# Padding three SBUF pools so that every tile that a matmul reads starts at a multiple of 256 bytes

## The chip, the cores and the metric

The kernel runs on 1 core of a Trainium2 chip. The metric is the device time of one execution in microseconds (us): 1028.81 us in the median of 3 runs (1028.7 to 1029.01). TensorE's clock has two levels, 1.2 and 2.4 GHz, which the profile shows as a granted clock of 0.5 and 1.0.

## The reference, cut to what matters

One layer of an encoder trunk on 512 tokens of width 1024, in float32, followed by a last RMSNorm. Every large product is a dense matmul:

```python
x = x + hybrid_mixer(rms_norm(x, norm_mix_g[l]), ...)          # p = h @ w_in (1024 x 7168), three gated branches, @ w_out
x = x + memory_cross_attention(rms_norm(x, norm_xa_g[l]), mem, ...)  # 4 heads of 256 into 256 memory tokens
x = x + swiglu(rms_norm(x, norm_ffn_g[l]), ...)                # (silu(h @ w_gate) * (h @ w_up)) @ w_down, hidden width 2816
return rms_norm(x, final_g)
```

## The kernel before, in words

A float32 product is made of three passes in the type float32r. An operand v is kept as two float32r tiles, hi (v rounded) and lo = v - hi, and `gemm` (L129 to L135) issues hi*hi, hi*lo and lo*hi into one PSUM tile. Each pass is a matmul with a 128x128 stationary operand, loaded by a weight load of its own (PEld in the profile), and a moving operand that streams 128 rows by N columns, N being 512 nearly everywhere. A moving column is 4 bytes in each of the 128 partitions, so a moving operand of 512 columns is a run of 2048 bytes in each partition, and a stationary one a run of 512.

The work goes through these stages, in program order, and TensorE's order is the program's:

- load and first norm, the values v of the attention (matmuls `pv`, N = 256);
- q and k (`pq`), the convolution branch (`pc`) and the attention heads (`z`), interleaved;
- the spatial gating (`pn`), then the gated branches (`pgt` and `pbr`);
- the projection back (`pb`, class `Back`), keys and values of the memory (`pk`, N = 256, and `pn`), cross attention (`pq`, `sc` with N = 256, `po`), `pb` again;
- the feed-forward part: the first columns with N = 256 (`pf`), then `pfg` and `pfu`, then `pb` for the down projection.

There are two forms of these products. In `col_gemm` (L137: `pq`, `pc`, `pgt`, `pfg`, `pfu`, `pk`, `pf`) a piece of a weight (`wh`, `wl`) is stationary and activations (`hT`, `h2`, `h3`, `mT`) move. In `nat_gemm` (L142: `pn`) and `Back` (L543 on: `pb`) activations (`hT`, `mT`, `mt`, `oT`, `aT`) are stationary and a weight piece of [128, 2, 512] moves. Transposes (L191, L401, L687, L498) are matmuls of 128 columns in plain float32, whose moving operand is the constant `ident`.

A weight is loaded by one DMA of SP's queue into a raw tile (`load_raw`, L107, two buffers) and split by ACT (hi, L100) and DVE (lo, L101) into `wh` and `wl`, five buffers each (`cut`, L112). These loads and splits run ahead of TensorE.

SBUF is given out by tile pools. Pools without a side are a stack that grows from low addresses, those with `side="right"` a stack that grows down from the top. Each tile takes its bytes in each partition, rounded up to a multiple of 32. The order of the pools on the left is `cst` (constants), `wp` (weights), `sm` (statistics), then the pools of each stage, opened and closed as the work goes on. `cst` starts at byte 16,512, and its tiles take 512 (`ident`), 32 (`mhalf`, one element), 512 (`zero`) and 192 (`chan`) bytes; so `wp` starts at 17,760, which is 96 bytes past a multiple of 256. `wp` takes 57,344 bytes, a multiple of 256, and `sm` 1,344, so that what follows starts at 76,448, 160 past one. The right side ends 32 bytes below the end of SBUF, at 229,344, and its tiles start 224 past a multiple of 256. Every address that a matmul reads keeps these remainders, as the steps inside the tiles are multiples of 512 bytes:

| tiles | bytes past a multiple of 256 |
|---|---|
| `wr`, `wh`, `wl` (weights) | 96 |
| `hT`, `h2`, `h3`, `mT`, `kx`, `vx`, `ya`, `yb`, `yc`, `vv`, `qk`, `kh`, `vl`, `ws` | 160 |
| `mt`, `oT`, `aT`, `qx`, `pT`, `es` (right side) | 224 |
| `ab`, `ah`, `al` (after the 1,284-column tile `om` in the pool `sk`) | 192 |
| `ident` | 128 |

In the pool `sk`, two tiles have a width that isn't a multiple of 64 elements: `om` (ZC + 4 = 1,284 columns, L382) and `y` (T + 2 = 514 columns, L355).

The instructions' order is made by the tile framework from the program and the tiles' dependencies. A tile that lies where a closed pool's tile lay waits for the last use of that one.

Of the kernel before, what the change touches and what calls it, by code (L numbers as in the profile page):

```python
# [17 lines left out]
def encoder_kernel(  # L18
# [6 lines left out]
):  # L25
    """Float32 products run as float32r passes: an operand v is kept as hi, v rounded to 12
    significant bits, and lo = v - hi, which is exact; hi*hi + hi*lo + lo*hi."""
    nc = tc.nc
# [36 lines left out]

# [1 line left out]
    ident = cst.tile([P, P], F32, name="ident")  # L67
# [4 lines left out]
    nc.vector.memset(zero, 0.0)  # L72
    # per-channel vectors, a row tile of 128 channels a column: four norm gains, three conv taps; spatial biases
    NC_ = 4 * KD + 3 * CT + CT
    WARM = 24
    chan = cst.tile([P, NC_], F32, name="chan")
    G_MIX, G_XA, G_MEM, G_FFN, C_W, B_S = 0, KD, 2 * KD, 3 * KD, 4 * KD, 4 * KD + 3 * CT

# [1 line left out]
    psx = {"i": 0, "pools": [(ps, "mm", 2)]}  # L80
# [16 lines left out]
    def split(src, hi, lo, scale=None):  # L97
        """hi = src rounded to float32r, lo = src - hi."""
        if scale is None:
            nc.scalar.copy(out=hi, in_=src)  # L100
            nc.vector.tensor_tensor(out=lo, in0=src, in1=hi, op=ALU.subtract)  # L101
        else:
            nc.scalar.activation(out=hi, in_=src, func=AF.Copy, scale=scale)
            nc.vector.scalar_tensor_tensor(out=lo, in0=src, scalar=scale, in1=hi,
                                           op0=ALU.mult, op1=ALU.subtract)
# [12 lines left out]
    def w_cols(w, c0, k0=0, k=KD, n=256):  # L118
        """Stationary weight: rows k0*128.., columns c0..c0+n, as n/128 tiles [128, k, 128]."""
        raw = load_raw(w[k0 * P:(k0 + k) * P, c0:c0 + n].rearrange("(k p) n -> p k n", p=P), k, n)  # L120
        return [cut(raw, (slice(None), slice(None), slice(j * P, (j + 1) * P)), k, P)
                for j in range(n // P)]

    def w_rows(w, k0, k, c0):
        """Moving weight: k row tiles from k0, 512 columns, as k/2 tiles [128, 2, 512]."""
        raw = load_raw(w[k0 * P:(k0 + k) * P, c0:c0 + 512].rearrange("(k p) n -> p k n", p=P), k, 512)
        return [cut(raw, (slice(None), slice(2 * j, 2 * j + 2)), 2, 512) for j in range(k // 2)]

    def gemm(dst, lh, ll, rh, rl, ks, first=True, last=True):  # L129
        """dst += sum over k of (lh+ll)[k].T @ (rh+rl)[k]; ks: pairs of indices."""  # L130
        n, tot = 0, 3 * len(ks)
        for a, b in ((lh, rh), (lh, rl), (ll, rh)):
            for i, j in ks:
                nc.tensor.matmul(dst, a(i), b(j), start=first and n == 0, stop=last and n == tot - 1)  # L134
                n += 1  # L135

    def col_gemm(dst, w, act, cs, k=KD):  # L137
        """dst[n, t] = w.T @ act: w = (hi, lo) [128, k, 128], act = (hi, lo) [128, k, T]."""
        gemm(dst, lambda i: w[0][:, i, :], lambda i: w[1][:, i, :],
             lambda i: act[0][:, i, cs], lambda i: act[1][:, i, cs], [(i, i) for i in range(k)])  # L140

    def nat_gemm(w, col0, act, ntt, evac):  # L142
        """out[t, n] for 512 columns of w."""
        pieces = []
        for c in range(2):
            pieces += w_rows(w, 4 * c, 4, col0)
        for t in range(ntt):
            dst = bank(nm("pn"))
            gemm(dst,
                 lambda i: act[0][:, i, t * P:(t + 1) * P], lambda i: act[1][:, i, t * P:(t + 1) * P],  # L150
                 lambda i: pieces[i // 2][0][:, i % 2, :], lambda i: pieces[i // 2][1][:, i % 2, :],
                 [(i, i) for i in range(KD)])
            evac(t, dst)
# [13 lines left out]
    def square_half(np_, key, xt, half):  # L167
        """Sum of squares of a half of a token tile's channels; with the second half, both summed."""
        junk = np_.tile([P, 512], F32, name=nm("jk"), tag="jk")
# [15 lines left out]
    def norm_turn(np_, h, g0, dst, t):  # L185
        """Transposes a token tile, applies the gain, splits into dst[:, :, token tile t]."""
        for g in range(2):
# [9 lines left out]

    # ================= mixer =================
    hp = pool("hp")
# [4 lines left out]
    sb = pool("sb")  # L204
    # v of a head: 64 columns hi, 64 columns lo
    vv = sb.tile([P, NT, W // HD, 2, HD], F32R, name="vv")
# [51 lines left out]

    # keeps the tensor engine's clock up while the first loads are under way
    warm = bank("warm")  # L260
# [32 lines left out]

    # key blocks (transposed) and query blocks (natural), packed to 1280 columns without crossing a bank
    OFF = {0: 0, 1: 512, 3: 896, 2: 1024}
    QOF = {3: 0, 2: 512, 0: 896, 1: 1024}
    ZC = 1280
    # one where no factor stands between s and t: s >= t - 1
    emask = sk.tile([P, ZC], F32, name="emask")
# [10 lines left out]
    def qk_jobs(c, got):  # L310
        """q and k, transposed, of two head pairs: four jobs."""
        held = {}

        def job(which, j):
# [3 lines left out]
            col_gemm(dst, held[which][j], hT, ALLT)  # L318
            # of the two heads in dst, each with its hi part on its own rows of qs, lo on the other head's;
            # ks the other way round, so that one product of 128 rows gives hi*lo + lo*hi  # L320
            st = sk.tile([P, 2, T], F32R, name=nm("qk"), tag=f"qk{which}", bufs=2)
# [17 lines left out]
    def conv_jobs(c):  # L339
        """The convolution branch for 256 channels: six jobs."""  # L340
        held, ccs, tmps = {}, [], []

        def job(which, j):
# [10 lines left out]
            elif which == 1:  # L354
                y = sk.tile([P, T + 2], F32, name=nm("y"), tag="y", bufs=1)  # L355
                nc.gpsimd.memset(y[:, 0:2], 0.0)
                nc.vector.tensor_tensor(out=y[:, 2:], in0=dst, in1=ccs[j], op=ALU.mult)
                tm = sk.tile([P, T], F32, name=nm("tm"), tag="tm", bufs=2)
                nc.scalar.activation(out=tm, in_=y[:, 2:], func=AF.Copy, scale=tap(2))
                nc.vector.scalar_tensor_tensor(out=tm, in0=y[:, 1:T + 1], scalar=tap(1), in1=tm,  # L360
# [12 lines left out]
    def sb_weights(par, q, k):  # L373
        """a[t, s] of a head, query block by query block: sig(z_ts) times the product of 1 - sig(z_tj), s < j < t."""
        r = HEAD[par]
        z = psz.tile([P, 1536], F32, name=nm("z"), tag="z", bufs=2)
        for i, o in QOF.items():
# [3 lines left out]
            mm(z[:, o:o + n], q[0][:, par, qi], k[0][:, par, 0:n], False, True)  # L381
        om = sk.tile([P, ZC + 4], F32, name=nm("om"), tag="om", bufs=1)  # L382
        nc.gpsimd.memset(om[:, ZC:ZC + 4], 1.0)
# [13 lines left out]
    def sb_turn(z, ab):  # L397
        """a transposed, key block by key block, in two parts."""
        for i in range(NT):
# [8 lines left out]
    def sb_values(pair, par, z, ah, al):  # L408
        r = HEAD[par]
        n_ = 0  # L410
        for i in range(NT):
            st = vv[:, i, 2 * pair + par].rearrange("p a d -> p (a d)")
            for b in (ah, al):
                mm(z[:, i * P:512], st, b[:, OFF[i]:OFF[i] + (NT - i) * P], n_ == 0, n_ == 2 * NT - 1)
                n_ += 1
        # v hi's rows and v lo's rows, summed
        yl = sk.tile([P, T], F32, name=nm("yl"), tag="yl", bufs=1)
# [32 lines left out]

# [1 line left out]
    yb_p = pool("ybp")  # L452
# [32 lines left out]
    for g in range(CT):  # L485
        gs = slice(g * P, (g + 1) * P)
        dst = bank(nm("pg")).rearrange("p (n c) -> p n c", n=NT)
        gemm(dst, lambda i: ws[0][:, g, :], lambda i: ws[1][:, g, :],
             lambda i: vl[0][:, :, gs], lambda i: vl[1][:, :, gs], [(0, 0)])
        # (mixed + bias) * u, in place of u  # L490
        nc.vector.scalar_tensor_tensor(out=un[:, :, gs], in0=dst, scalar=chan[:, B_S + g:B_S + g + 1],
                                       in1=un[:, :, gs], op0=ALU.add, op1=ALU.mult)
# [10 lines left out]

# [1 line left out]
    mtp = pool("mtp", side="right")  # L505
# [32 lines left out]

    # ================= residual, projections back to the model width =================
    xp = pool("xp")  # L540
    xr = [xp.tile([P, D], F32, name=f"xr{t}") for t in range(NT)]

    class Back:  # L543
        """xr[t] += act.T @ w. Halves of 512 columns; in the second one the last `tail` row tiles go
        token tile by token tile."""

# [81 lines left out]

    # memory keys and values
    for c in range(4):  # L630
# [12 lines left out]

    # ================= cross attention =================
    op_ = pool("op", side="right")
# [78 lines left out]

    # ================= feed forward =================
    # the first 256 columns start with the first two token tiles
    HT = (slice(0, T // 2), slice(T // 2, T))
# [55 lines left out]
    close(psm)  # L783
    close(ps)
    close(sm)
    close(wp)
# [30 lines left out]
```

## Time and profile before

| | |
|---|---|
| median of 3 runs | 1028.81 us (1028.7 to 1029.01) |
| profiled execution, its own time (span from the first to the last instruction) | 1028.6 us |
| PE, PEld, DVE, ACT, POOL busy | 98%, 81%, 44%, 37%, 8% of the span |
| DMA | 100.65 MB, mean 98 GB/s |
| granted clock of TensorE, mean | 0.994 |

How to read it: PE is TensorE's matmuls, PEld its weight loads, which overlap the matmuls. A matmul's end is modelled, and its duration holds the time in the pipeline, so the mean duration of a matmul (some 390 ns) isn't the time that it takes from the next one; that is the distance between starts, which the chain of waits gives for a run of equal matmuls as its length divided by its count.

### The profile page before, as it was taken

The numbers are of one execution on the slowest core, as the hardware profiler recorded it, in microseconds if no ns is written. First come the engines' busy times: TensorE is split into PE (matmuls) and PEld (weight loads), VectorE is DVE, ScalarE is ACT, GpSimd is POOL, SyncE is SP. The second block draws the span as 40 slices with busy tenths as digits, with TensorE's granted clock in tenths as the row PEclk, the third lists the DMA queues.
The fourth block names the chain that finished last, engine by engine and source line by source line (L and its number), as shares of the span: only waits on it lengthen the run. The fifth ranks groups of instructions, "written<-read, shape, count | busy, mean of one in ns | idle before, by whom it ended". The sixth has DMA issues, their size and how long they took to land.

```text
span 1028.6 us, 11686 instructions
## 1 busy us (share of the span) xinstructions
PE 1012.3 (98%) x4826; PEld 836.7 (81%) x4826; DVE 454.5 (44%) x576; ACT 381.7 (37%) x541; POOL 86.2 (8%) x115
## 2 busy tenths in 40 slices
PE   7999999999999999999999999999999999999997
PEld 7978778887888888888888887988888888888885
DVE  6576687545332323346745443643333333322213
ACT  5464554334222223345534433542332322312211
POOL 1121122130001212120000000000000000000000
PEclk8999999999999999999999999999999999999999
DMA  7312212123223232360544121232322322323202
GB/s 246 116 59 72 82 50 100 46 83 123 83 80 123 83 123 64 101 244 25 182 137 149 41 82 41 83 124 84 121 82 86 120 82 87 120 81 122 82 21 83
DMA packets 77334, 100.65 MB, mean 98 GB/s; under 512 B 1905, under 2 KB 57249, under 8 KB 77281
## 3 DMA queue, kind: packets, MB, share of 16 engines
q1 hardware_dynamic: 76032, 95.45, 28.4%
q0 software_dynamic: 1248, 4.46, 1.2%
q8 instruction: 38, 0.62, 0.3%
q14 instruction: 16, 0.12, 0.0%
HBM read 97.80 MB, written 2.10 MB: 97 GB/s over the span
## 4 chain that ended last, share of the span: by engine, by line
PE 95%; DMA 1%; ACT 1%; DVE 1%; issue 1%; SPq 0%; POOL 0%; DVEq 0%; POOLq 0%; ACTq 0%
PE pb L134 20%; PE pgt L134 13%; PE pfg L134 11%; PE pfu L134 11%; PE pq L134 8%; PE pn L134 7%; PE pc L134 6%; PE pbr L134 6%; PE z L371 3%; PE pv L134 2%; PE pf L134 2%; PE pk L134 1%; PE po L134 1%; PE sc L134 1%; PE pt L191 1%; PE z L401 1%
## 5 line engine op out<-in xcount | busy, mean ns | idle before, releaser
L101 DVE TENSOR_TENSOR wl<-wr,wh 128x1024 fp32r<-128x1024 f32 x174 | 213.1, 1229 | 304.2 <-ACT wh L100 150.9
L100 ACT CAST wh<-wr 128x1024 fp32r<-128x1024 f32 x174 | 181.2, 1048 | 369.6 <-PE pb L134 87.4
L134 PE MATMUL pb<-wh,aTh 128*128 128x512 f32 x176 | 55.2, 395 | 0.0
L134 PE MATMUL pb<-wl,aTh 128*128 128x512 f32 x176 | 55.2, 395 | 0.0
L134 PE MATMUL pb<-wh,aTl 128*128 128x512 f32 x176 | 55.2, 395 | 0.0
L759 DVE TENSOR_TENSOR fs<-pfu,fs 128x512 f32<-128x512 f32 x20 | 13.8, 692 | 85.4 <-PE pfu L134 85.4
L134 PE MATMUL pgt<-hTh,wh 128*128 128x512 f32 x192 | 47.9, 392 | 0.0
L134 PE MATMUL pgt<-hTl,wh 128*128 128x512 f32 x192 | 47.9, 392 | 0.0
L134 PE MATMUL pgt<-hTh,wl 128*128 128x512 f32 x192 | 47.8, 391 | 0.0
L162 POOL TENSOR_TENSOR rs<-ve,mhalf 128x1 f32<-128x1 f32 x22 | 14.4, 657 | 381.8 <-DVE ve L160 369.4
L531 POOL TENSOR_TENSOR merged<-merged,sg 128x512 f32<-128x512 f32 x16 | 27.7, 1731 | 184.8 <-DVE sg L530 184.8
L134 PEld LDWEIGHTS pgt<-hTh,wl 128*128 128x128 f32 x192 | 36.1, 188 | 8.0
L134 PEld LDWEIGHTS pgt<-hTl,wh 128*128 128x128 f32 x192 | 36.1, 188 | 7.9
L134 PEld LDWEIGHTS pgt<-hTh,wh 128*128 128x128 f32 x192 | 36.0, 188 | 7.9 <-DVE ybl L101 0.2
L134 PE MATMUL pfg<-h3h,wh 128*128 128x512 f32 x160 | 40.0, 391 | 0.0
L134 PE MATMUL pfg<-h3l,wh 128*128 128x512 f32 x160 | 39.9, 392 | 0.0
L134 PE MATMUL pfu<-h3l,wh 128*128 128x512 f32 x160 | 39.9, 392 | 0.0
L134 PE MATMUL pfu<-h3h,wh 128*128 128x512 f32 x160 | 39.9, 391 | 0.0
L134 PE MATMUL pfu<-h3h,wl 128*128 128x512 f32 x160 | 39.8, 391 | 0.0
L134 PE MATMUL pfg<-h3h,wl 128*128 128x512 f32 x160 | 39.8, 391 | 0.0
L134 PEld LDWEIGHTS pb<-wh,aTh 128*128 128x128 f32 x176 | 33.0, 188 | 8.1
L134 PEld LDWEIGHTS pb<-wh,aTl 128*128 128x128 f32 x176 | 33.0, 188 | 8.0
(240 smaller groups left out, 1824.6 us busy)
## 6 DMA issues: line engine op xcount, KB each, us to landing
wr<-in_w_in_dram SPq DMA_DIRECT2D x26, 1024.0 KB, 5.1
wr<-in_w_gate_ffn_dram SPq DMA_DIRECT2D x11, 1024.0 KB, 5.4
wr<-in_w_up_ffn_dram SPq DMA_DIRECT2D x11, 1024.0 KB, 5.3
wr<-in_w_down_ffn_dram SPq DMA_DIRECT2D x10, 1024.0 KB, 4.9
wr<-in_w_branch_dram SPq DMA_DIRECT2D x6, 1024.0 KB, 5.2
wr<-in_w_out_dram SPq DMA_DIRECT2D x4, 1024.0 KB, 5.0
wr<-in_w_k_xa_dram SPq DMA_DIRECT2D x4, 1024.0 KB
wr<-in_w_v_xa_dram SPq DMA_DIRECT2D x4, 1024.0 KB, 5.7
```

The costliest lines, as they stand in the source:

```text
L100: nc.scalar.copy(out=hi, in_=src)
L101: nc.vector.tensor_tensor(out=lo, in0=src, in1=hi, op=ALU.subtract)
L134: nc.tensor.matmul(dst, a(i), b(j), start=first and n == 0, stop=last and n == tot - 1)
L162: nc.gpsimd.tensor_tensor(out=rs, in0=ve, in1=mhalf, op=ALU.pow)
L191: nc.tensor.transpose(pt[:, j * P:(j + 1) * P], h[:, d * P:(d + 1) * P], ident)
L371: mm = lambda dst, a, b, st, sp: nc.tensor.matmul(dst, a, b, start=st, stop=sp, skip_group_check=True)
L401: nc.tensor.transpose(z[:, OFF[j] + (i - j) * P:OFF[j] + (i - j + 1) * P], ab[:, QOF[i] + j * P:QOF[i] + (j + 1) * P], ident)
L531: nc.gpsimd.tensor_tensor(out=merged[:, d, :], in0=merged[:, d, :], in1=sg, op=ALU.add)
L759: nc.vector.tensor_tensor(out=sg, in0=pu, in1=sg, op=ALU.mult)
```

## The change

Three tiles are added that nothing writes or reads: `cpad` (40 elements, 160 bytes) at the end of `cst`, `spad` (48 elements, 192 bytes) in `sm`, and `rpad` (56 elements, 224 bytes) in a new pool `rp`, the first on the right side. `om` and `y` get a width that is a multiple of 64 elements; the columns that are used stay the same. The rest of the diff takes out comments and docstrings.

```diff
     chan = cst.tile([P, NC_], F32, name="chan")
+    cst.tile([P, 40], F32, name="cpad")
+    sm.tile([P, 48], F32, name="spad", bufs=1)
+    rp = pool("rp", side="right")
+    rp.tile([P, 56], F32, name="rpad")
...
-                y = sk.tile([P, T + 2], F32, name=nm("y"), tag="y", bufs=1)
+                y = sk.tile([P, T + 64], F32, name=nm("y"), tag="y", bufs=1)
                 nc.gpsimd.memset(y[:, 0:2], 0.0)
-                nc.vector.tensor_tensor(out=y[:, 2:], in0=dst, in1=ccs[j], op=ALU.mult)
+                nc.vector.tensor_tensor(out=y[:, 2:T + 2], in0=dst, in1=ccs[j], op=ALU.mult)
                 tm = sk.tile([P, T], F32, name=nm("tm"), tag="tm", bufs=2)
-                nc.scalar.activation(out=tm, in_=y[:, 2:], func=AF.Copy, scale=tap(2))
+                nc.scalar.activation(out=tm, in_=y[:, 2:T + 2], func=AF.Copy, scale=tap(2))
...
-        om = sk.tile([P, ZC + 4], F32, name=nm("om"), tag="om", bufs=1)
+        om = sk.tile([P, ZC + 64], F32, name=nm("om"), tag="om", bufs=1)
...
+    close(rp)
```

With 160 bytes more, `cst` ends at 17,920 = 70 x 256; `sm` with 192 more is 1,536 = 6 x 256 bytes; the right side starts at 229,120 = 895 x 256. `om` takes 5,376 = 21 x 256 bytes and `y` 2,304 = 9 x 256.

## Rows read from the trace of the kernel before

**Rows 1.** The page: the first line, busy time by engine, the granted clock in 40 slices, and the chain of waits by engine.

```profile
span 1028.6 us, 11686 instructions
PE 1012.3 (98%) x4826; PEld 836.7 (81%) x4826; DVE 454.5 (44%) x576; ACT 381.7 (37%) x541; POOL 86.2 (8%) x115
PEclk8999999999999999999999999999999999999999
PE 95%; DMA 1%; ACT 1%; DVE 1%; issue 1%; SPq 0%; POOL 0%; DVEq 0%; POOLq 0%; ACTq 0%
```

**Rows 2.** The chain of waits in order of time, pieces of it: start us, length us, what and how many instructions.

```profile
431.03 5.49 PE pgt L134 x24
436.52 2.75 PE pbr L134 x12
439.27 22.40 PE pb L134 x96
...
514.10 22.40 PE pn L134 x96
536.50 11.20 PE pq L134 x48
...
591.85 11.00 PE pq L134 x48
...
887.40 5.49 PE pfg L134 x24
892.89 5.50 PE pfu L134 x24
898.39 123.21 PE pb L134 x528
```

**Rows 3.** The first 30 us: a part of the windows' table (stretch, its length, PE busy with its count, granted clock, DMA share, GB/s), and pieces of the chain.

```profile
13.00:17.00 4.00, 4.00 (x19) 0.50 0.50 175
...
2.57 7.43 DMA wr<-in_w_in_dram
...
18.73 5.46 PE pv L134 x48
24.19 0.87 PE pt L191 x8
```

**Rows 4.** Timeline of PE in the stretch 5 to 18.8 us (start, length, line, operation, out<-in, shape, count): two runs of `pv` matmuls of 256 columns.

```profile
14.73 1.91 PE L134 MATMUL pv<-wl,hTh 128*128 128x256 f32 x8
16.44 1.41 PE L134 MATMUL pv<-wh,hTl 128*128 128x256 f32 x8
```

**Rows 5.** Timeline of PE about 112 us: one attention head's products with the values, whose moving tiles `ah` and `al` lie 192 past a multiple of 256.

```profile
111.37 0.39 PE L371 MATMUL z<-ah,vv 128*128 128x512 f32 x1
111.60 0.39 PE L371 MATMUL z<-al,vv 128*128 128x512 f32 x1
111.83 0.34 PE L371 MATMUL z<-ah,vv 128*128 128x384 f32 x1
112.00 0.34 PE L371 MATMUL z<-al,vv 128*128 128x384 f32 x1
```

**Rows 6.** How many matmuls there are: the windows' table over the whole span for one tile at a time, in the order `pb`, `pn`, `pgt` (16 transposes of L498 among them), `pfg`, `pfu`, `pc`, `pq`, `pbr`, `po` (512 columns each) and `pk`, `pf`, `pv`, `sc` (256 columns).

```profile
0.00:1028.60 1028.60, 216.60 (x912) 0.99 0.30 98
0.00:1028.60 1028.60, 67.97 (x288) 0.99 0.30 98
0.00:1028.60 1028.60, 138.43 (x592) 0.99 0.30 98
0.00:1028.60 1028.60, 113.30 (x480) 0.99 0.30 98
0.00:1028.60 1028.60, 113.13 (x480) 0.99 0.30 98
0.00:1028.60 1028.60, 68.45 (x288) 0.99 0.30 98
0.00:1028.60 1028.60, 90.93 (x384) 0.99 0.30 98
0.00:1028.60 1028.60, 69.84 (x288) 0.99 0.30 98
0.00:1028.60 1028.60, 11.68 (x48) 0.99 0.30 98
0.00:1028.60 1028.60, 22.98 (x192) 0.99 0.30 98
0.00:1028.60 1028.60, 23.77 (x192) 0.99 0.30 98
0.00:1028.60 1028.60, 25.51 (x192) 0.99 0.30 98
0.00:1028.60 1028.60, 13.35 (x96) 0.99 0.30 98
```

**Rows 7.** The windows' table by stage: busy time and count of PE, PEld, DVE, ACT and POOL, then granted clock, DMA share and GB/s.

```profile
60.00:200.00 140.00, 140.00 (x647) 111.24 (x646) 99.23 (x93) 73.13 (x85) 24.60 (x47) 1.00 0.23 73
...
240.00:440.00 200.00, 200.00 (x876) 163.94 (x877) 68.58 (x74) 61.29 (x73) 27.75 (x19) 1.00 0.31 100
...
900.00:1028.00 128.00, 121.59 (x522) 97.46 (x520) 34.00 (x43) 23.38 (x33) 2.20 (x4) 0.98 0.23 78
```

## The prediction

> **What bounds the kernel now.** I read the page first: TensorE is busy for 98% of the span of 1028.6 us, and PE holds 95% of the chain of waits that ended last, DMA, ACT and DVE 1% each [rows 1]. The granted clock is 1.0 but for the first slice [rows 1]. So the time is the sum of the distances between matmul starts, and nearly no wait is left to shorten. The question of this change is what one such distance is, and whether it depends on addresses.
>
> The chain in order of time answers the first half, as length over count. In the form with moving activations the distance is 5.49 / 24 = 228.8 ns (`pgt`, `pfg`), 5.50 / 24 = 229.2 (`pfu`) and 2.75 / 12 = 229.2 (`pbr`); in the form with moving weights it is 22.40 / 96 = 233.3 (`pb`, `pn`) and 123.21 / 528 = 233.4 (`pb`) [rows 2]. 512 columns at one column per cycle of 2.4 GHz are 213.3 ns, so each such matmul costs 15.5 to 20 ns more than its columns.
>
> Two more views say what kind of excess that is. At the granted clock of 0.50, which is 1.2 GHz [rows 3], the start of the second run of eight `pv` matmuls of 256 columns lies 16.44 - 14.73 = 1.71 us after the first's [rows 4]: 213.8 ns each, where the columns alone are 256 / 1.2 = 213.3. So at the lower clock there is no excess. At the full clock 48 of the same shape take 5.46 us [rows 3], 113.8 ns each, against 106.7. And it grows with the columns: 384 columns take (112.00 - 111.83) = 0.17 to 0.18 us against 160 ns, 512 take (111.83 - 111.37) / 2 = 230 ns [rows 5]. It is thus a limit on how fast the moving operand comes at 2.4 GHz, about one cycle in 11 to 15, and no fixed price of an instruction. A plain float32 transpose, which takes two cycles a column, has nearly none of it: 0.87 / 8 = 108.8 ns against 106.7 [rows 3].
>
> **The change, part by part.** It adds no instruction and no DMA, and no engine's work gets longer: the padding is never touched, and the used columns of `om` and `y` stay as they were. The instructions, their order and their queues should be those of before. What moves are addresses, all of them.
>
> *Moving and stationary operands.* The price of an aligned operand isn't in the trace: by the table of addresses no moving float32r operand starts at 0 or 128 past a multiple of 256. It is bounded by rows. Below, the excess goes and only the transposes' 2.1 ns stay: 213.3 + 2.1 = 215.4 ns for 512 columns, 106.7 + 2.1 = 108.8 for 256. Above, all go at the slowest rate seen, 233.4. The counts are 912 + 288 = 1200 for moving weights and 576 + 480 + 480 + 288 + 384 + 288 + 48 = 2544 for moving activations (the 16 transposes of `pgt` left out), and 192 + 192 + 192 + 96 = 672 of 256 columns [rows 6]. At the low end the change gives back 1200 x (233.3 - 215.4) = 21.5 us, 2544 x (229.0 - 215.4) = 34.6 us and 672 x (113.8 - 108.8) = 3.4 us: 59.5 us. At the high end it costs 2544 x (233.3 - 229.0) = 10.9 us.
>
> I take zero, and the reason is in rows with the same and with different addresses. Moving `h2` from the same addresses (160 past), against stationary weights at 96, `pq` takes 11.20 / 48 = 233.3 ns in one stretch and 11.00 / 48 = 229.2 in a later one [rows 2]. The slow stretch begins where `pn`, itself at 233.3, ends without a gap (514.10 + 22.40 = 536.50) [rows 2]. So there are two rhythms in which matmuls and their weight loads run, and a stream stays in the one that it comes from; the address doesn't choose. And `ah` and `al`, at 192 past and so the only moving float32r tiles that start at a multiple of 64, take 230 ns [rows 5], no less than those at 160. A penalty for starting off a boundary of 64 would have vanished there. What stays possible is a boundary of 128 or 256, which no row tests.
>
> [...]
>
> *DMA, ACT and DVE.* Their tiles move as well. DMA is on the chain with about 1% (10 us, of which one load takes 7.43 [rows 3]), ACT and DVE with 1% each [rows 1]. Were each a tenth faster or slower, that is 3 us either way; I take zero. In the stages they are covered: between 60 and 200 us, the densest, DVE is busy 99.23 of 140 us, and in the last, DVE 34.00 of 128 [rows 7], so a slowing that stays under 40% in the first doesn't reach TensorE by itself.
>
> *Waits.* The two stacks come 576 bytes closer together (352 and 224), and tiles inside a stack keep their order, so each lies over the same closed tiles, and I expect no new wait. None is added by the diff.
>
> The sum is 0: a profiled span of 1028.6 us; the median of the runs stands 0.2 above it at 1028.8.
>
> **Rivals.**
>
> *The excess is straddling.* If the moving operand is fetched in units of 128 or 256 bytes that now straddle two, the excess goes with the alignment: 1028.8 - 59.5 = 969 us, 970 with a little lost where ACT and DVE come closer to being late (99.23 in a stage that would shrink from 140 to about 132 [rows 7]). For it: the excess grows with the bytes moved, it is absent when the stream is half as fast [rows 4], and no tile of before is aligned. Against it: remainders of 96, 160 and 192 all cost about the same [rows 2, 5], where one would expect straddling to differ between them.
>
> *All in the fast rhythm.* If the moving weights' remainder of 96 is what puts `pb` and `pn` into the slow one, they fall to 228.9: 1200 x 4.4 = 5.3 us less, 1023.5. For it: this form is slow wherever it appears, and returns to it after `pbr` at 229.2 [rows 2]. Against it: `pq` was slow without that remainder.
>
> *All in the slow rhythm.* With every operand at the same place within 256 bytes, a moving read and the weight load beside it (PEld is busy for 81% of the span [rows 1]) start in step, and the streams that now escape to 229 hold at 233.3 as `pq` did after `pn`: 10.9 us more, 1039.7. It decides from the point at which `pgt` and `pfg` take 5.60 us for 24. Against it: `pgt`, `pfg` and `pfu` keep the fast one through whole stages.
>
> **How the numbers follow.** Forecast, no change: 0.45, at 1028.8, within 1026 to 1032. Straddling: 0.32 at 970. All fast: 0.08 at 1023.5. All slow: 0.15 at 1039.7. A measurement of this kernel can tell 0.2%, 2 us, from no change. The forecast splits by the 3 us for the other engines into 0.04 faster, 0.33 same and 0.08 slower, so faster has 0.04 + 0.32 + 0.08 = 0.44 and slower 0.08 + 0.15 = 0.23. The range reaches down past the straddling case to 966 and up to 1034, short of the all slow case, leaving out some 0.16.
>
> **What would show it.** Right: `pgt` at 5.49 for 24 and `pb` at 123.2 for 528, the same counts of instructions, the same chain. Straddling shows as `pgt` near 5.17 for 24 and `pb` near 114 for 528. Another rhythm shows in `pb` alone (120.9) or in `pgt` alone (5.60). The prediction is wrong if either group leaves its rate by more than 1 ns a matmul, or if a new wait shows between stages.

## The result, and the profile after

The changed kernel takes 1015.75 us in the median of 4 runs (1014.83 to 1018.19), the kernel before 1028.76 beside it: the ratio is 0.9886, with an interval of 0.9869 to 0.9902. Run a second time, it took 1017.71 against 1028.09, ratio 0.9895 (0.9877 to 0.9913). So the change is worth 10 to 13 us.

The page after, the same lines as [rows 1]:

```profile
span 1014.0 us, 11686 instructions
PE 1000.7 (99%) x4826; PEld 837.5 (83%) x4826; DVE 455.1 (45%) x576; ACT 382.5 (38%) x541; POOL 86.3 (9%) x115
PEclk9999999999999999999999999999999999999999
PE 95%; DMA 2%; DVE 1%; ACT 1%; issue 0%; SPq 0%; DVEq 0%; POOLq 0%; ACTq 0%
```

The counts of instructions are those of before on every engine, and ACT, DVE and POOL are busy for the same time within 0.8 us. PE alone lost 11.6 us. The chain of waits in order of time shows how; the lines answer to [rows 2], and the last three to matmuls of 256 columns:

```profile
210.28 21.81 PE pn L139 x96
...
425.48 5.44 PE pgt L139 x24
...
433.63 21.77 PE pb L139 x96
...
506.71 21.79 PE pn L139 x96
528.49 10.88 PE pq L139 x48
...
583.26 10.88 PE pq L139 x48
...
881.87 5.44 PE pfu L139 x24
887.31 119.69 PE pb L139 x528
...
16.29 5.75 PE pv L139 x48
...
646.63 8.51 PE pf L139 x71
660.31 9.60 PE pf L139 x80
```

Every long run of products of 512 columns now has one rate: 5.44 / 24 = 226.7 ns, 21.79 / 96 = 227.0, 10.88 / 48 = 226.7, 119.69 / 528 = 226.7, where [rows 2] had 229 and 233.3. At the granted clock 0.5, 256 columns of `pv` take 213.4 ns from start to start (mean of 12, this profile) and 512 of `pgt` take 426.7 (the run with the order alone, below): 0.833 ns a column and nothing beside it. The trace gives the clock as a granted share alone; 1.2 and 2.4 GHz are what these times come to at one column a cycle and at twice that clock. Half the time, at the granted clock 1.0, is 213.3 ns for 512 columns, so that at 226.7 each matmul still costs 13.4 ns more than its columns. The 256 columns got slower: 5.75 / 48 = 119.8 ns against 5.46 / 48 = 113.8 [rows 3]. That is 13.1 ns over their 106.7, and the 384 columns of the products with `ah` and `al` take 173.2 ns from start to start (mean of 16), 13.2 over their 160 (128 columns of `ah`: 62.4, 9 over 53.3, from eight matmuls). So what stays at the full clock is the same for 256, 384 and 512 columns: a price of each matmul, and no longer one that grows with its columns. The feed-forward's first part, in the kernel before:

```profile
655.96 8.37 PE pf L134 x71
...
669.45 9.42 PE pf L134 x80
```

goes from 8.37 to 8.51 us for 71 and from 9.42 to 9.60 for 80.

The account, summed from the starts of all matmuls in the two traces: `pb` and `pn` went from 280.9 us to 273.7, 7.2 less; the other products of 512 columns took 5.5 us less; those of 256 columns 1.4 us more (some 2 by their rates at the full clock, but fewer of them ran at the lower one). That is about 11 us net. The rest of the 14.6 us between the two profiled spans (1028.6 and 1014.0) is two waits that also differ between executions of one kernel, as the runs below show. The wait ahead of `pk` is 1.5 us shorter, and the first `pv` starts at 10.71 us, where it was 12.86; from the two chains, before and after:

```profile
12.86 4.99 PE pv L134 x24
...
10.71 4.34 PE pv L139 x24
```

### The profile page after: what moved, and what is told of

Its sections match the earlier page's. It is cut to its first block, busy times and chain, and to the rows that moved or that the text cites. A ratio compares the mean times of both kernels' runs of the same rounds, so it can differ in the third digit from the quotient of the medians.

```text
span 1014.0 us, 11686 instructions
## 1 busy us (share of the span) xinstructions
PE 1000.7 (99%) x4826; PEld 837.5 (83%) x4826; DVE 455.1 (45%) x576; ACT 382.5 (38%) x541; POOL 86.3 (9%) x115
## 4 chain that ended last, share of the span: by engine, by line
PE 95%; DMA 2%; DVE 1%; ACT 1%; issue 0%; SPq 0%; DVEq 0%; POOLq 0%; ACTq 0%
PE pb L139 20%; PE pgt L139 13%; PE pfg L139 11%; PE pfu L139 11%; PE pq L139 8%; PE pc L139 7%; PE pn L139 6%; PE pbr L139 6%; PE z L376 3%; PE pv L139 2%; PE pf L139 2%; PE pk L139 1%; PE sc L139 1%; PE po L139 1%; PE pt L196 1%; PE z L406 1%
## 5 line engine op out<-in xcount | busy, mean ns | idle before, releaser
L139 PEld LDWEIGHTS pb<-wl,aTh 128*128 128x128 f32 x176 | 33.0, 188 | 6.9
```

## The experiments

With the changed kernel alone one can't say which of three things did it: that the addresses are multiples of 256 (or of 64), that the moving and the stationary operand now have the same remainder, or that the moving one alone is aligned. I write d for the moving operand's remainder of 256 minus the stationary one's. Before, d was 64 in the form with moving activations, -64 in `pn`, 128 in `pb`.

**The pad in the constants alone.**

```diff
-    sm.tile([P, 48], F32, name="spad", bufs=1)
-    rp = pool("rp", side="right")
-    rp.tile([P, 56], F32, name="rpad")
...
-    close(rp)
```

> Only the pad in the constants stays: weights at 0, stage tiles (hT, h2, h3, y, ...) at 64, right side at 224 past a multiple of 256. Theory A (both operands have to start at a multiple of 64): pgt and pfg 5.44 us for 24 (226.7 ns), pb, whose stationary tiles lie at 224, stays at 233 ns (123 us for the last 528); time near 1021. Theory B (moving and stationary need the same remainder of 256): nothing is at 226.7; pgt 228.8 to 233, time 1026 to 1035. Theory C (multiples of 256 for both): as B. Theory D (the moving operand alone, multiple of 64): pgt and pb both at 226.7, time near 1015.

Measured: 1029.31 us, the kernel before beside it 1026.37. Chain of waits:

```profile
211.84 22.40 PE pn L136 x96
...
429.41 5.49 PE pgt L136 x24
...
534.76 11.21 PE pq L136 x48
...
564.38 2.80 PE po L136 x12
567.18 10.99 PE pq L136 x48
...
897.40 123.19 PE pb L136 x528
```

`pgt` has its moving tiles at 64 and its stationary ones at 0, both multiples of 64, and still takes 228.8 ns; `pb` moves from 0 over 224, and takes 233.3. Theories A and D fall. In these groups the rate goes with d: `pgt` has 64 as before and its rate of before, `pn` has -64 as before and keeps 22.40 / 96 = 233.3, and `po`, whose stationary tile went from 160 to 64 past under a moving one that stayed at 224 (d from 64 to 160, which is -96 within 256), went from the fast rate to 2.80 / 12 = 233.3. `pq` shows that d isn't all: with d = 64 throughout it takes 11.21 / 48 = 233.5 behind `pn` and 10.99 / 48 = 229.0 later, as it did in [rows 2].

**All at 32**, and **all at 64**: the pads with other sizes; at 32 as below, at 64 the pad in the constants has 56 elements and that on the right side 40.

```diff
-    cst.tile([P, 40], F32, name="cpad")
+    cst.tile([P, 48], F32, name="cpad")
-    rp.tile([P, 56], F32, name="rpad")
+    rp.tile([P, 48], F32, name="rpad")
```

> The three pads are kept with other sizes, so that every tile that a matmul reads lies at 32 past a multiple of 256. Theory A (multiples of 64) and C (multiples of 256): no group at 226.7, pgt 5.49 to 5.60 us for 24, pb 123 us for 528, time 1027 to 1038. Theory B (same remainder): all at 226.7 as in the changed kernel, time near 1015. Theory D (moving at a multiple of 64): as A.

> As the changed kernel, with every such tile at 64 past a multiple of 256. Theories A, B and D: all groups at 226.7 (pgt 5.44 us for 24, pb 119.7 for 528), time near 1015. Theory C (multiples of 256): pgt at 5.49 or above, pb near 123, time 1027 or above.

Measured: 1020.0 us at 32 and 1016.74 at 64. From the chain of waits at 32:

```profile
427.32 5.44 PE pgt L139 x24
...
891.60 119.69 PE pb L139 x528
```

At 64:

```profile
427.09 5.44 PE pgt L139 x24
...
888.33 119.69 PE pb L139 x528
```

Both have the rates of the changed kernel to the hundredth of a microsecond. No multiple of 256 is needed, nor of 64: equal remainders are enough. Of the 3.3 us between the two runs, 3.0 come between the `pgt` and the `pb` shown: about 498 us the first one waits 1.8 us ahead of `pk`, the second 0.2, and the first one's clock then falls to the lower level for a while (stretch, its length, PE busy, granted clock, DMA share, GB/s, at 32):

```profile
480.00:495.00 15.00, 15.00 (x118) 1.00 0.53 166
495.00:502.00 7.00, 5.16 (x32) 0.76 0.72 246
```

**Weights back at 96, all else at 0.**

```diff
-    cst.tile([P, 40], F32, name="cpad")
-    sm.tile([P, 48], F32, name="spad", bufs=1)
+    sm.tile([P, 24], F32, name="spad", bufs=1)
```

> Weights stay at 96 past a multiple of 256, as before the change; stage tiles and right side lie at 0. Theory A and C (both operands aligned): no product with a weight is at 226.7; only po, pg and the attention's values, which have no weight, are; time 1026 to 1033. Theory B (same remainder): as A. Theory D (the moving operand alone): pgt, pfg, pq, pc at 226.7 (5.44 us for 24), pb and pn, where the weight moves, at 233; time near 1022. And if the weights' DMA is faster at multiples of 256 of SBUF, the first load of weights on the chain falls back from 5.3 us to about 7 and the median landing of 1 MB from 5.0 to 5.3 us in this run, and not in the run with the constants alone.

Measured: 1042.93 us, 16.6 more than the kernel before beside it (1026.37). Chain of waits:

```profile
428.97 5.62 PE pgt L138 x24
...
911.03 123.22 PE pb L138 x528
```

`pgt`, whose moving tiles are at multiples of 256 now, runs at 234.2 ns, the slowest rate of a whole group. That is d = -96. So aligning all pools but that of the weights costs 16.6 us here (one run of each; the kernel before took 1026.4 to 1031.3 in all its runs), and aligning that one too gains some 11 over before. The median landing of the gate weights was 5.4 us, against 5.1 with the constants alone, which goes the way expected. The first load, 6.17 us, tells nothing: on the chains here it takes 5.3 to 7.7 us (the run with the order alone has one of 8.3 us from 5.47 us in its place), and differs between two profiles of one kernel as much as between kernels.

**Differences of 32**: weights at 32, stage tiles at 0, the right side at 64.

```diff
-    cst.tile([P, 40], F32, name="cpad")
+    cst.tile([P, 48], F32, name="cpad")
-    sm.tile([P, 48], F32, name="spad", bufs=1)
+    sm.tile([P, 40], F32, name="spad", bufs=1)
-    rp.tile([P, 56], F32, name="rpad")
+    rp.tile([P, 40], F32, name="rpad")
```

> Pads of other sizes: weights at 32, stage tiles at 0, right side at 64 past a multiple of 256. So the moving operand lies 32 bytes below the stationary one's remainder in pgt, pfg, pq, pc, pbr (0 - 32) and in pb (32 - 64), 32 above it in pn (32 - 0) and 64 above it in po. Theory B (the difference of the two remainders sets the rate) with 226.7 at difference 0 alone: pgt and pb both lose the rate of 226.7 and stand between 229 and 234, and show the same rate although their addresses differ; pn 233.3 as the pb of the run with the constants alone (0 - 224 = 32); po 229 to 230 as before (224 - 160 = 64). Rival (each operand's own address counts): pgt, whose moving tiles lie at 0, keeps 226.7.

Measured: 1037.6 us, before 1029.5. Chain of waits:

```profile
426.96 5.60 PE pgt L139 x24
432.56 2.80 PE pbr L139 x12
...
905.68 123.21 PE pb L139 x528
...
568.59 2.75 PE po L139 x12
```

`pgt` (0 over 32) and `pb` (32 over 64) have the same d = -32 at different addresses and the same 233.3 ns; `po`, d = 64, has 2.75 / 12 = 229.2 as `pbr` had at d = 64 in [rows 2]. So where a whole group has one difference, the rate goes with it and not with the single addresses.

**Differences below 32 bytes**: hT, h2 and h3 as views that start inside a wider tile, at elements 44 and 52 in the first run, at 47 and 50 in the second.

```diff
+        for s, o in (("h", 44), ("l", 52)):
+            f = p.tile([P, KD * T + 64], F32R, name=f"{name}{s}")
+            got.append(f[:, o:o + KD * T].rearrange("p (k t) -> p k t", k=KD))
...
-    hT = tuple(hp.tile([P, KD, T], F32R, name=f"hT{s}") for s in "hl")
+    hT = shifted(hp, "hT")
```

> The kernel before, with hT, h2 and h3 shifted inside their tiles by 176 bytes (hi) and 208 bytes (lo), so that in pgt, pfg, pfu, pq and pc the moving hi lies 16 bytes below the stationary weight's remainder of 256 and the moving lo 16 bytes above it; pb and pbr keep their addresses of before. If equality is needed to less than 16 bytes: 229 to 234 ns for both, pgt 5.49 to 5.62 us for 24. If a coarser agreement is enough (the same 32 or 64 bytes): 226.7, 5.44. pb stays at 233.3 either way.

> As the run with 16 bytes, with the moving hi 4 bytes below the weight's remainder and the moving lo 8 bytes above. If only an exact match counts: 229 to 234 ns. If it is the agreement of a 16-byte piece or of something near: 226.7 for at least one of the two, pgt 5.44 us for 24 or close to it.

Measured: 1035.01 and 1032.47 us, before 1029.5. Chain of waits, first run and second:

```profile
425.26 5.57 PE pgt L134 x24
...
433.05 5.56 PE pgt L134 x24
```

The three passes, as means of the distance from one start to the next in the trace:

```
pgt, moving hTh (stationary wh)   d = -16: 233.0 ns     d = -4: 230.0 ns
pgt, moving hTl (stationary wh)   d = +16: 230.6 ns     d = +8: 233.3 ns
pgt, moving hTh (stationary wl)   d = -16: 233.3 ns     d = -4: 231.8 ns
```

Four bytes, one element, already lose the rate. Of all the differences tried, only equality gives 226.7. But where differences alternate, as here, d alone doesn't give the rate. In the `pn` of the first run, two passes with d = +16 take 228.2 ns and the one with d = -16 takes 230.2, less than the same differences take in `pgt`, where -16 has two passes of three. And `pb`, expected at 233.3 with its addresses of before, takes 122.7 / 528 = 232.4 in both runs.

**The kernel before, a second time.**

> The kernel before, unchanged, profiled a second time. If the first weight load of 7.43 us and the wait of 2.6 us ahead of the memory's keys (pk) belong to the addresses, they come back within 0.3 us; if they are chance of one execution, they differ by 0.5 us or more. The rates come back: pgt 5.49 us for 24, pb 123.2 for 528.

Measured: 1028.88 us. Chain of waits:

```profile
2.58 7.39 DMA wr<-in_w_in_dram
...
431.24 5.49 PE pgt L134 x24
...
896.94 123.21 PE pb L134 x528
```

The rates come back to the digit, and the first load does (7.39 against 7.43). The wait ahead of `pk` doesn't: 1.3 us, where the first profile had 2.4. Nor does the slow stretch of `pq` behind `pn`, which the prediction had used: all of `pq` with h2 runs at 229.0 ns this time. The run with the constants alone, with the same d of 64, had it again. So at d = 64 the stream can run in either rhythm.

**The changed kernel, a second time.**

> The changed kernel, unchanged, a second time. The rates come back: pgt 5.44 us for 24, pb 119.7 for 528, time 1013 to 1018. If the earlier start of the first values' matmuls (10.7 us, with a first weight load of 5.3 us on the chain) belongs to the addresses, it comes back within 0.3 us; if it is chance, it lies between 11 and 13 us, as in the other runs.

Measured: 1017.71 us, the ratio given above. Chain of waits:

```profile
2.57 7.10 DMA wr<-in_w_in_dram
...
12.54 4.77 PE pv L139 x24
...
427.38 5.44 PE pgt L139 x24
...
889.98 119.69 PE pb L139 x528
```

The rates come back, the early start doesn't: `pv` starts at 12.54 us. The 2.15 us of the first profile were chance; the 11 us of the rates are the change.

**Which stationary operand counts**: lo weights at 64, passes interleaved; and the interleaved order alone.

```diff
+        if not wpad:
+            wpad.append(wp.tile([P, 16], F32, name="wpad", bufs=1))
         l = wp.tile([P, a, b], F32R, name=nm("wl"), tag="wl", bufs=5)
...
-        for a, b in ((lh, rh), (lh, rl), (ll, rh)):
-            for i, j in ks:
+        for i, j in ks:
+            for a, b in ((lh, rh), (ll, rh), (lh, rl)):
```

(`spad` is 16 elements smaller in the first, so that the stage tiles stay at 0; the second has the last hunk alone.)

> The changed kernel with the lo parts of the weights at 64 past a multiple of 256, all else at 0, and the three passes interleaved: for each row tile hi*hi, lo*hi, hi*lo, so that stationary wh and wl alternate. Theory N (what counts is the remainder of the weight load that runs beside the matmul, the next one's): in pgt and pfg the matmuls with hTh and wh, whose next load is wl, take 231 to 235 ns from start to start, the other two kinds 226 to 228; 24 take near 5.50 us. Theory O (the matmul's own stationary operand counts): the matmuls with wl take 231 to 235, the other two 226 to 228. If the streams hold one rhythm across matmuls, all three change alike. pb, where wl moves over stationary tiles at 0, goes up for the wl matmuls in both, to 229 or more.

> The changed kernel with the three passes interleaved and nothing else changed: the control for the run with the lo parts at 64. All at equal remainders, so 226.7 ns for all three kinds, pgt 5.44 us for 24, pb 119.7 for 528, time 1013 to 1018, if the order plays no part.

Measured: 1035.28 us with the lo parts at 64, 1022.59 with the order alone. Chain of waits, first and second:

```profile
428.90 5.55 PE pgt L141 x24
...
903.72 122.51 PE pb L141 x528
...
425.85 5.44 PE pgt L139 x24
...
893.88 119.69 PE pb L139 x528
```

The order alone keeps the rates of the changed kernel, and yet its span is 3.9 us longer than in that one's second profile. It loses 1.4 us ahead of the first `pq` (41.80 us on the chain, 40.44 there) and waits 2.7 us for DVE's `ybl` ahead of the first `pgt`. Twice, from 139.5 us and, behind that wait, from 245.3 us, its granted clock is 0.5 for 3.4 us. On the other side it has no wait ahead of `pk` (1.7 us there).

Means of the distances in the trace, by the matmul's own stationary operand and the next one's in `pgt`, by the moving one in `pb`:

```
pgt                          lo at 64    order alone
hTh over wh, next is wl       229.0        226.9
hTh over wl, next is wh       236.0        226.2
hTl over wh, next is wh       228.3        227.0
pb
wh over aTh                   232.5        227.0
wh over aTl                   231.3        227.0
wl over aTh                   232.2        226.0
```

In `pgt` theory O is nearer: the matmul whose own stationary operand lies elsewhere is the slow one, while the one beside which a load from there runs is not. But its neighbours lose 2 ns too, so it isn't a price of single matmuls; the stream keeps part of it. And this rests on a recorded start being the moment at which a matmul's stream begins; if the records run one matmul early or late, own and next change places.

`pb` and `pn` speak against both theories. There the `wl` matmuls have d = 64 and the `wh` ones d = 0, and all three kinds of `pb` take 231 to 233 ns: the ones with equal remainders are as slow as their neighbours, and the mixture is slower than d = 64 is by itself (229). That is the third case of the expectation, one rhythm for all. So equal remainders bring 226.7 ns where the matmuls around have them too, as in the changed kernel and in the runs at 32 and at 64, and a stream that alternates between two differences has a rate of its own. The order by itself plays no part in the rates.

**Another difference for the 256 columns.**

```diff
+    kvp.tile([P, 48], F32, name="kpad")
     kx = tuple(kvp.tile([P, KD, NM], F32R, name=f"kx{s}") for s in "hl")
+    kvp.tile([P, 16], F32, name="vpad")
...
+    mp.tile([P, 48], F32, name="mpad")
     mT = tuple(mp.tile([P, KD, NM], F32R, name=f"mT{s}") for s in "hl")
```

> The changed kernel with the memory's tiles kx and mT at 192 past a multiple of 256, so that in the products of 256 columns sc and pk the moving operand lies 64 below the stationary one's remainder, where 113.7 to 114 ns a matmul were seen, against 119.7 at equal remainders. If the best difference for 256 columns is another than for 512: pk (192 matmuls) and sc (96) take 6 ns less each, 1.7 us, and the memory's pn (96 matmuls, stationary 64 below the moving) 2.3 ns more, 0.2 us: 1.5 us less than the changed kernel in the same job, about what the intervals can show. If not, pk stays at 119.7.

Measured: 1016.53 us (1016.22 to 1017.76), ratio 0.9893 (0.9879 to 0.9908), against 0.9895 for the changed kernel beside the same runs of the kernel before. Chain of waits:

```profile
497.24 11.58 PE pk L139 x96
508.81 11.23 PE pn L139 x49
```

The same 96 of `pk` take 11.78 us in the changed kernel's second profile, so 2 ns a matmul were gained and not 6 (both pieces hold short waits; the means from start to start are 117.7 and 119.9 ns). The `pn` in this line went to 229.2, as foreseen for d = 64. So for 256 columns d alone doesn't set the rate: d = -64 gave 113.7 in `pv` of the first experiment and 117.7 here, and in the kernel before, d = 64 gave 115.6 in `pk` and 117.8 in `pf`. Nothing measurable is left in it.

## Why the prediction was right or wrong

*What bounds the kernel* held: the time is the sum of the distances between starts, and the rates that changed are TensorE's. That there is an excess at the granted clock 1.0 and none at 0.5 holds too (at equal remainders, 512 columns of `pgt` at 0.5 take 426.7 ns from start to start in the run with the order alone, 256 of `pv` 213.4 in the first profile after: twice the columns in twice the time). That it grows with the columns and is "no fixed price of an instruction" was a fair reading of the rows of before, but it isn't so at equal remainders, where 13 ns are left for 256, 384 and 512 columns alike. For 256 columns that is more than the 7 to 11 ns of before, so they got slower.

*The change part by part* held for the instructions, for ACT and DVE, and for the waits: counts and order of the stages are the same, and no new wait appeared. The step that failed is "I take zero", with its reason "the address doesn't choose". The address does choose, but not as an operand's alignment: I looked at whether each operand starts on a boundary, compared 160, 192 and 96 one by one, and found nothing, as there is nothing. What counts is the pair: at equal remainders both forms take 226.7 ns (0, 32 and 64 past alike), where d = 64 had 228.9 and d = -64 and 128 had 233.3. The rows had it in sight: before the change no product with weights had equal remainders, and the two rates went with d = 64 against d = -64 and 128. `ah` and `al`, taken as the test of a boundary, stand at d = 32 over `vv`; their 512 columns went from 231.9 ns (mean of 16) to 227.1. The one piece of evidence that spoke against addresses, `pq` at 233.3 and later at 229.2 from the same ones, shows that a stream can stay for a while in the rhythm of what ran before it. It didn't come back in the second profile and did in the run with the constants alone. That part of the reasoning holds. The step from it to "the address doesn't choose" doesn't: two rates at one d don't show that all differences have these two.

*The rivals.* Straddling, 970, fell: at 32 past a multiple of 256 the rate is the same as at 0, and no run came near 215 ns. "All in the fast rhythm" had the right kind of result, both forms at one rate, and the right term for `pb` and `pn` (5.3 us foreseen, 7.2 measured), but took 228.9 as the floor; the 2.2 ns below it on the other 2544 matmuls bring 5.5 us, and the 256 columns cost 1.4, which no case had. "All in the slow rhythm", with operands that start in step, was the reverse of what happens: in step is best, and 234.2, the slowest rate of a whole group with one difference, came from tiles at 0 over weights at 96.

*The numbers.* 1015.75 lies in the range by luck: it was wide because of the straddling case, and the result falls between the cases that I had priced; 1028.8, no change, was given the largest chance and was wrong by 13 us. Faster had 0.44, the largest of the three.

*DMA* was taken as zero, rightly for the time. The loads did change a little: the median landing of the gate weights (1 MB each) is 5.0 to 5.2 us in the six profiles with the raw weight tiles at multiples of 256, and 5.3 to 5.6 in the eight others. The address that a load writes is what moved; why it should change the landing, no run shows. It is hidden behind TensorE, which is busy for 98% of the span before and 99% after.

*What stays open* is the mechanism. In the `pgt` of the interleaved run the load beside a matmul isn't what slows it (228.3 and 229.0 ns over `wh`, the latter with the next load from `wl`, against 236.0 over `wl` itself); its `pb` can't tell. The difference of the two streams' addresses is worth 3% of a matmul (233.3 against 226.7 ns), and how it comes to that, no run shows. Why a mixture of differences is slower than its parts, and what the 13 ns are that each matmul still costs at equal remainders, wasn't found.

## What to carry to other kernels

In float32r products with a weight load each, give the moving and the stationary tiles the same remainder of 256 bytes, whichever it is (0, 32 and 64 were tried): in this kernel 512 columns then take 226.7 ns, and 228 to 236 ns otherwise. Do it for all tiles that follow one another on TensorE or not at all: aligning all pools but the weights' made this kernel 16.6 us slower, and with only the lo weights elsewhere the products whose remainders were equal lost the rate as well; and look at the addresses again whenever a small tile is added to a pool that lies below the large ones, because 32 bytes there move everything above it. When a trace has only a few combinations of two addresses, tabulate pairs before saying that addresses don't matter.

## What the runs showed of the hardware that was not expected

In passes that have one difference d, the rate of 512 columns goes with it, and finely: 226.7 ns at 0, 229 at 64 (233 in some stretches), 233.3 at -64, 32 either way, 96 and 128, 234.2 at -96 (233.3 in `po`). The differences 64 and -64 don't behave alike. Where passes of two differences alternate, -4 took 230 to 232, 8 and -16 233, 16 231 in `pgt`. Where d alternates from matmul to matmul, matmuls at d = 0 took 228 to 229 between ones at -64, and 231 to 233 between ones at 64. At equal remainders each matmul costs 13 ns more than its columns at the full clock, for 256, 384 and 512 columns alike, and none at the lower one (512 in 426.7 ns, 256 in 213.4). For 256 columns equality is among the slowest cases, 119.8 ns, as is d = 96 (119.9 in `pv` with the weights at 96); the fastest was `pv` at d = -64, 113.5 to 113.8 in the kernel before and with the constants alone.
